# The second layer's latent projection as three passes of high and low parts with 512 weight columns streaming

## The chip, the cores and the metric

The kernel runs on one core of a Trainium2 chip. The metric is device time in microseconds (us) of one execution, the median of several. Five engines work side by side, each through its own instructions in order: PE (TensorE, matrix products into PSUM; PEld are its weight loads), DVE (VectorE), ACT (ScalarE), POOL (GpSimd, which issues the gathers) and SP (SyncE, which issues most loads).

## The reference, cut to what matters

Two transformer-like layers are run for two groups that share all weights: 128 context tokens (block 0) and 256 latent tokens (blocks 1 and 2). D is 1024, everything is float32. In each layer

```
h   = LN(x) * (1 + scale1) + shift1
q_a, k_a, v_a, cq, ckv, krope, u_c, v_c = split(h @ w_in)      # 1024 x 1696, the projection
q_a = rms(q_a) * g;  k_a = rms(k_a) * g;  latent tokens also get a rotary turn (rope)
mix = concat(GQA 8 heads, latent attention (MLA) 4 heads, gated MLP) @ w_o
x   = LN(alpha * x + gate1 * mix)
x   = LN(alpha * x + gate2 * PEER(LN(x) * (1 + scale2) + shift2))
```

PEER scores 16 x 128 keys per token (`h2 @ peer_wq`, queries), takes the best pairs (routing) and mixes 128 of 16384 single-neuron experts. For the latent tokens the kernel runs all experts densely on PE; for the context tokens it gathers the chosen rows of two tables.

## The kernel before, in words

Tokens stand 128 to a partition block. A layer has two stages. The first is attention: the latent chain (`lat`, blocks 1 and 2) and the context chain (`cc`, block 0) run interleaved. Each does: LN and transpose (`transposed_mod`, L193, gives `hT`, the transposed h, 8 chunks of 128 x 128 per block), projection (`project`, L247), attention (L341), output projection (`out_proj`, tiles `psoc`, `psol`), LN. The context chain then runs its queries (L552, tile `psqp`), routing (L573) and 128 + 128 gathers (L679) with a DVE product for each gathered row. The second stage is the dense expert work of the latent tokens (L852 and L926, tiles `psA` and `acc`), with the context's gathers spread between.

`project` before: the 1696 columns of `w_in` come in 13 strips of 128 and one of 32. A strip is one load of 128 x 1024 float32 (all 8 chunks of the contraction, 128 columns each) into one of `RB` = 6 ring buffers that all loads on SP share. For each block, 8 float32 matmuls (L262, the transposed h stationary, the 128 weight columns streaming) sum into one PSUM bank (`psil` for the latent blocks, `psic` for the context), and ACT copies the strip out to `proj` (L263). So after five strips the 640 columns of q and k are there, and `norm_qk` (L295: square on ACT, sum, reciprocal root, three products, rope on DVE) can start on them.

The ring buffer of a strip comes free when the matmuls of both blocks have read it. The context chain of the second layer has a small ring of its own (`cr1`, two buffers).

The order on each engine is not the order of the code: a list scheduler (`schedule_with_timeline_sim`, L1119) places instructions by priority and by its own simulated times, and `hp()` gives the context chain a higher priority. `ORD1` ('paol...') sets the code order: the context's projection, attention and output projection first, then the 14 steps of the latent projection, to which the scheduler gives the gaps. The latent attention's tiles lie in a pool `lb1` that is opened on the right-hand side of SBUF after the projection's code.

The dense expert stage already splits float32 numbers into a high part (a copy to the type float32r, ACT) and a low part (the difference, DVE) and does three matmuls in place of one: high by high, low by high, high by low (L915, L916, L926).

Of the kernel before, what the change touches and what calls it, by code (L numbers as in the profile page):

```python
# [8 lines left out]
F32 = mybir.dt.float32  # L9
F32R = mybir.dt.float32r  # L10
# [3 lines left out]
AF = mybir.ActivationFunctionType  # L14
# [10 lines left out]
IN_W = sum(SIZES)  # L25
# [20 lines left out]
def tile_fn(ctx: ExitStack, tc, A, outs):  # L46
    nc = tc.nc
    V, S, T = nc.vector, nc.scalar, nc.tensor
# [23 lines left out]
    def run(g, n=None):  # L72

        for k, _ in enumerate(g):
            if n is not None and k + 1 == n:
                return
# [170 lines left out]
    def project(l, ch):  # L247

        ch.hT = {b: ch.P.tile([128, 8, 128], F32, name=f"hT{b}", tag=f"hT{i}") for i, b in enumerate(ch.bs)}
        for b in ch.bs:  # L250
            with crit(b):
                transposed_mod(b, l, 1, 0, lambda h: ch.hT[b][:, h * 4:h * 4 + 4, :], "m1", ch.P, ch.tT)
        ch.proj = {b: ch.P.tile([128, IN_W], F32, name=f"proj{b}", tag=f"proj{i}") for i, b in enumerate(ch.bs)}
        for j in range(14):
            w0 = j * 128
            n = min(128, IN_W - w0)
            wv = load(A["w_in"][l, :, w0 * 8:(w0 + n) * 8], f"wi{ch.g}{j}", n * 8, ch.cring)
            wv = wv.rearrange("p (c n) -> p c n", c=8)
            for b in ch.bs:
                ps = pS(ch.tS, "psi" + ch.g)  # L260
                for c in range(8):
                    T.matmul(ps[:, :n], lhsT=ch.hT[b][:, c, :], rhs=wv[:, c, :], start=(c == 0), stop=(c == 7))  # L262
                S.activation(ch.proj[b][:, w0:w0 + n], ps[:, :n], AF.Copy)  # L263
            if j == 9 and ch.ctxg:
                p0 = ch.proj[0]
                nc.scalar.dma_start(o_v[0, l].rearrange("s k d -> s (k d)"), p0[:, O_V:O_V + 128])
                nc.scalar.dma_start(o_kr[0, l], p0[:, O_KR:O_KR + 32])
            yield j

    class Chain:  # L270

# [478 lines left out]
    for l in range(DEPTH):  # L750
        last = l + 1 == DEPTH

        with ExitStack() as es3:
            psum(es3, BK[min(l, 1)])
            with ExitStack() as esc:
                Pc = pool(esc, f"cb{l}")
                if l:
                    with hp():
                        ctx_close(l - 1, pk, Pc)
                Pl = pool(es3, f"lp{l}", side="right")  # L760
                Wl = Shared(l, Pc, Pl)
                if l:
                    Wl.load()
                lat = Chain(l, [1, 2], Pl, Wl)
                cc = Chain(l, [0], Pc, Wl, pool(esc, f"cr{l}") if l else None)
                pl_ = project(l, lat)
                def first():
                    run(project(l, cc))
                    if l == 0:
                        with tc.issue_after(hmark[-1].ins):  # L770
                            Wl.load()
                            for t, n in late:
                                nc.scalar.dma_start(t, A[n])

                st_ = {"p": first, "2": lambda: modulation(0, 2, "m"),
                       "4": lambda: modulation(0, 4, "m"), "3": lambda: modulation(0, 3, "m"),
                       "a": lambda: cc.attention_in(esc), "o": lambda: out_c(cc)}
                for k in (ORD if l == 0 else ORD1):
                    if k == "l":
                        run(pl_, 1)  # L780
                    else:
                        with hp():
                            st_[k]()
                with hp():
                    pk = ctx_picks(l, cc, esc)
                run(pl_)
                if not last:
                    mods = [(l + 1, v) for v in (1, 0, 2, 4, 3, 5)]
                    for _ in range(MB):
                        modulation(*mods.pop(0), "m")  # L790
                lat.attention(pool(es3, f"lb{l}", side="right"))
                lat.out_proj()
                if l == 0:
                    modulation(0, 5, "m")

        with ExitStack() as es_:
# [32 lines left out]
            for b in (1, 2):  # L829
# [3 lines left out]
                for h in range(2):  # L833
                    hs = slice(h * 4, h * 4 + 4)
# [97 lines left out]
            for b in range(2):  # L932
                g, i1, i2 = routing(l, vals[b], idx[b], PK, PK)
                ps = pS("t", "psr")
# [48 lines left out]
            for b in (1, 2):  # L983
# [3 lines left out]
                with crit():  # L987
                    for h in range(2):
                        hs = slice(h * 512, (h + 1) * 512)
# [7 lines left out]
            for k, r in RATES[l].items():  # L997
                ms = marks[k]
                n = int(len(ms) * r + 0.5)
# [47 lines left out]
def _layout(i):  # L1047
    import numpy as np
    i = {k: np.asarray(v) for k, v in i.items()}
    L = i["w_mod"].shape[0]  # L1050
    f = np.float32
    r = {}

    def chunks(w, n):
        k = w.shape[2] // n
        return w.reshape(L, 8, 128, k, n).transpose(0, 3, 2, 1, 4).reshape(L, k, 128, 8 * n)
# [10 lines left out]
    t = np.arange(256)  # L1067
# [20 lines left out]
    r["w_mod"] = i["w_mod"].reshape(L, 8, 128, 6, D).transpose(0, 3, 1, 2, 4)  # L1088
    wi = i["w_in"].reshape(L, 8, 128, IN_W).transpose(0, 2, 1, 3)
    r["w_in"] = np.concatenate([wi[:, :, :, j * 128:(j + 1) * 128].reshape(L, 128, -1) for j in range(14)], -1)  # L1090
    r["w_o"] = chunks(i["w_o"], 128)
    r["peer_wq"] = chunks(i["peer_wq"], 128)
    r["peer_uT"] = i["peer_u"].reshape(L, 128, 128, 8, 128).transpose(0, 1, 4, 3, 2).reshape(L, 128, 128, 1024)
# [29 lines left out]
```

## Time and profile before

| | us |
|---|---|
| three runs | 2402.37, 2407.3, 2410.01 |
| median | 2407.3 |
| the profiled execution, its own time | 2407.9 |
| its span | 2406.1 |
| PE busy | 2260.6 (94%) |
| DVE busy | 1904.6 (79%) |
| ACT busy | 1115.2 (46%) |

The second layer's projection of both chains runs from about 1222 to 1342 us of the span, the rest of the attention stage to about 1500, and the expert stage from there to the end. A row of a timeline gives start, duration, engine, line, operation, tile and its inputs, shape, count, and in brackets the idle time ahead of it; a row by stretch gives the stretch, its length, the busy us (and records) of PE, PEld, DVE, ACT and POOL, PE's granted clock, the DMA share and GB/s. A matmul of float32 shows as two records in the trace. Matmuls are pipelined, so the durations of single records overlap; the chain of waits gives the time that a group of them takes one after the other. Busy PE is time with a matmul in flight, at whatever pace.

### The profile page before, as it was taken

How to read it: one execution, taken by the hardware profiler on the slowest of the kernel's cores; microseconds unless marked ns; L12 is line 12 of the kernel's file. 1: busy time of each engine (PE TensorE's matmuls, PEld its weight loads, DVE VectorE, ACT ScalarE, POOL GpSimd, SP SyncE). 2: the span in 40 equal slices, each digit the busy share in tenths (PEclk: the TensorE clock that was granted, in tenths of full speed). 3: DMA queues.
4: the chain of work that ended last, by engine and by line, in shares of the span. 5: the costliest groups of instructions: out<-in, count | busy, mean ns of one | idle time of the engine just before them, and what ended most of it. 6: DMA issues, size and time to landing. Idle time of an engine off the chain costs nothing.

```text
span 2406.1 us, 41658 instructions
## 1 busy us (share of the span) xinstructions
PE 2260.6 (94%) x15660; PEld 1914.5 (80%) x15660; DVE 1904.6 (79%) x3942; ACT 1115.2 (46%) x2084; POOL 697.7 (29%) x523
## 2 busy tenths in 40 slices
PE   6999889999999999999989996989999999998997
PEld 5686469999998995667778785889999889855886
DVE  3157579996898888898863468899879888899987
ACT  3324532442785445444445553134348744444444
POOL 0000233454004433464200003435530143344630
PEclk8999989999999999999999998999999999998998
DMA  9967889999658999999863355989985599987994
GB/s 331 322 193 265 336 322 348 324 358 350 219 159 295 360 332 347 328 352 374 299 213 113 120 158 196 325 313 349 363 320 159 188 374 346 333 309 270 395 364 147
DMA packets 196314, 696.05 MB, mean 289 GB/s; under 512 B 22992, under 2 KB 27408, under 8 KB 196112
## 3 DMA queue, kind: packets, MB, share of 16 engines
q1 hardware_dynamic: 110016, 398.52, 46.7%
q0 software_dynamic: 74736, 272.14, 31.1%
q10 hardware_dynamic: 11360, 22.73, 2.8%
q8 instruction: 123, 2.02, 0.3%
q14 instruction: 79, 0.65, 0.1%
HBM read 689.14 MB, written 4.16 MB: 288 GB/s over the span
## 4 chain that ended last, share of the span: by engine, by line
PE 32%; DVE 8%; issue 8%; DMA 2%; POOL 1%; ACT 1%; DVEq 0%; ACTq 0%; POOLq 0%
PE acc L926 18%; PE psA L852 6%; DVE gt L692 2%; PE psil L262 2%; DMA gt<-in_peer_u_dram,ids 1%; POOL gt L686 1%; PE psqp L561 1%; PE psic L262 1%; DVE ulo L847 1%; PE psoc L522 1%; PE pssl L421 1%; DMA wic<-in_w_in_dram 1%; PE psW L890 0%; DVE idx L550 0%; DVE rep L548 0%
## 5 line engine op out<-in xcount | busy, mean ns | idle before, releaser
L686 POOL DMA_INDIRECT gt<-in_peer_u_dram,ids x256 | 325.3, 1271 | 1185.6 <-DVE gt L692 478.4
L686 POOL DMA_INDIRECT gt<-in_peer_v_dram,ids x256 | 368.0, 1438 | 464.0 <-DVE acc L703 434.7
L926 PE MATMUL acc<-vhi,pp 128*128 128x512 f32 x1728 | 441.9, 398 | 15.6 <-ACT pp L906 9.4
L852 PE MATMUL psA<-h2hi,uhi 128*128 128x256 f32 x1664 | 416.2, 287 | 5.1 <-ACT uhi L846 5.1
L852 PE MATMUL psA<-h2lo,uhi 128*128 128x256 f32 x1664 | 411.3, 284 | 0.0
L926 PEld LDWEIGHTS acc<-vhi,pp 128*128 128x128 f32 x1728 | 326.1, 191 | 86.3 <-ACT pp L906 10.0
L915 ACT ACTIVATE vhi<-v 128x1024 fp32r<-128x1024 f32 x216 | 228.7, 1060 | 274.0 <-PE acc L926 161.2
L692 DVE SCALAR_TENSOR_TENSOR gt<-gt,h2c 128x1024 f32<-128x1024 f32 x256 | 309.5, 1216 | 28.0 <-DMA gt<-in_peer_u_dram,ids 27.9
L703 DVE SCALAR_TENSOR_TENSOR acc<-gt,wcol,acc 128x1024 f32<-128x1024 f32 x254 | 325.5, 1282 | 6.2 <-DMA gt<-in_peer_v_dram,ids 5.2
L846 ACT ACTIVATE uhi<-u 128x1024 fp32r<-128x1024 f32 x208 | 220.0, 1058 | 230.2 <-PE psA L852 107.5
L852 PEld LDWEIGHTS psA<-h2hi,uhi 128*128 128x128 f32 x1664 | 319.7, 192 | 7.9 <-ACT uhi L846 5.7
L852 PEld LDWEIGHTS psA<-h2lo,uhi 128*128 128x128 f32 x1664 | 320.0, 192 | 2.1
L847 DVE TENSOR_TENSOR ulo<-u,uhi 128x1024 fp32r<-128x1024 f32 x208 | 254.3, 1223 | 79.9 <-ACT uhi L846 74.7
L916 DVE TENSOR_TENSOR vlo<-v,vhi 128x1024 fp32r<-128x1024 f32 x216 | 263.6, 1223 | 52.6 <-ACT vhi L915 47.7
L852 PE MATMUL psA<-h2hi,ulo 128*128 128x256 f32 x1664 | 239.4, 286 | 1.0 <-DVE ulo L847 0.8
L926 PE MATMUL acc<-vlo,pp 128*128 128x512 f32 x864 | 234.3, 392 | 1.5 <-DVE vlo L916 1.4
L852 PEld LDWEIGHTS psA<-h2hi,ulo 128*128 128x128 f32 x1664 | 216.2, 192 | 3.0 <-DVE ulo L847 1.6
L872 ACT ACTIVATE e<-iota,nid 128x128 f16<-128x128 f16 x512 | 158.9, 426 | 112.1 <-PE psW L890 112.1
L926 PEld LDWEIGHTS acc<-vlo,pp 128*128 128x128 f32 x864 | 162.3, 189 | 35.8 <-DVE vlo L916 2.5
L852 PE MATMUL psA<-h2T,u 128*128 128x256 f32 x768 | 171.8, 379 | 0.0
L852 PEld LDWEIGHTS psA<-h2T,u 128*128 128x128 f32 x768 | 143.1, 190 | 18.1
L926 PE MATMUL acc<-v,AR 128*128 128x512 f32 x320 | 143.6, 599 | 0.0
(437 smaller groups left out, 3039.9 us busy)
## 6 DMA issues: line engine op xcount, KB each, us to landing
u<-in_peer_uT_dram SPq DMA_DIRECT2D x256, 512.0 KB, 6.0
v<-in_peer_v_dram SPq DMA_DIRECT2D x256, 512.0 KB, 6.0
wm<-in_w_mod_dram SPq DMA_DIRECT2D x96, 512.0 KB, 7.2
wq<-in_peer_wq_dram SPq DMA_DIRECT2D x64, 512.0 KB, 4.7
wic<-in_w_in_dram SPq DMA_DIRECT2D x26, 512.0 KB, 5.7
wil<-in_w_in_dram SPq DMA_DIRECT2D x26, 512.0 KB, 4.2
woc<-in_w_o_dram SPq DMA_DIRECT2D x16, 512.0 KB
wol<-in_w_o_dram SPq DMA_DIRECT2D x16, 512.0 KB, 3.6
```

Source lines behind the costliest of these rows:

```text
L262: T.matmul(ps[:, :n], lhsT=ch.hT[b][:, c, :], rhs=wv[:, c, :], start=(c == 0), stop=(c == 7))
L421: T.matmul(sb[i][:, m * nk:(m + 1) * nk], lhsT=lhs(i, h), rhs=rhs(h), start=True, stop=True)
L686: nc.gpsimd.indirect_dma_start(out=t, out_offset=None, in_=tab, in_offset=bass.IndirectOffsetOnAxis(ap=pk.ids[:, j:j + 1], axis=0))
L692: V.scalar_tensor_tensor(t, t, 1.0, pk.h2c, op0=OP.mult, op1=OP.mult, accum_out=acol[:, j:j + 1])
L703: V.scalar_tensor_tensor(pk.acc, t, wcol[:, j:j + 1], pk.acc, op0=OP.mult, op1=OP.add)
L846: S.activation(hi, ua, AF.Copy)
L847: marks["A" if ii < NA else "U" if ii < NA + PRE else "B"].append(V.tensor_sub(lo, ua, hi.bitcast(F32)))
L852: T.matmul(ps[:, a * 256:(a + 1) * 256], lhsT=lw[:, c * 128:(c + 1) * 128], rhs=rw[:, c, :], start=(k == 0), stop=(k == len(passes) - 1))
L872: S.activation(e2[:, t // TI, :, t % TI], iota1, AF.Abs, bias=nb_[:, t0 % 128 + t:t0 % 128 + t + 1])
L915: S.activation(hi, v, AF.Copy)
L916: marks["O" if ii >= NA else "Q" if ii >= NA - PRE else "P"].append(V.tensor_sub(lo, v, hi.bitcast(F32)))
L926: T.matmul(accp[tb][h], lhsT=pl[:, tb * 128:(tb + 1) * 128], rhs=vr[:, h * 512:(h + 1) * 512], start=st0, stop=sp)
```

## The change

Only the second layer's latent projection changes; the first layer and the context keep `project`. The new `project_split` takes the weights from a second copy `w_in5` in DRAM, laid out in three groups of 512 columns and one of 160. A load brings two chunks of the contraction by 512 columns (128 x 1024), or four chunks by 160 (128 x 640). For the groups of 512 the load is split into `wjhi` (ACT copy to float32r) and `wjlo` (DVE difference), two buffers each, and the transposed h into `hThi` and `hTlo`. For each chunk and block three matmuls of 512 streaming columns follow (high h by high w, low h by high w, high h by low w), and the sum of all eight chunks is copied out in one piece of 512 columns per block. The last 160 columns stay float32. The new tiles lie in a pool `pj1` on the right-hand side that is closed before `lb1` is opened, so that `lb1` takes its place.

```diff
+    def project_split(l, ch, P2):
+        ch.hT = {b: ch.P.tile([128, 8, 128], F32, ...) for i, b in enumerate(ch.bs)}
+        hl = {}
+        for b in ch.bs:
+            with crit(b):
+                transposed_mod(b, l, 1, 0, lambda h: ch.hT[b][:, h * 4:h * 4 + 4, :], "m1", ch.P, ch.tT)
+                hi = P2.tile([128, 8, 128], F32R, name=f"hThi{b}")
+                lo = P2.tile([128, 8, 128], F32R, name=f"hTlo{b}")
+                for h in range(2):
+                    hs = slice(h * 4, h * 4 + 4)
+                    S.activation(hi[:, hs], ch.hT[b][:, hs], AF.Copy)
+                    V.tensor_sub(lo[:, hs], ch.hT[b][:, hs], hi[:, hs].bitcast(F32))
+                hl[b] = (hi, lo)
...
+        for q in range(4):
+            w0, n, m = q * 512, (512 if q < 3 else IN_W - 1536), (2 if q < 3 else 4)
+            ps = {b: pS(t, "psi" + ch.g) for b, t in zip(ch.bs, (ch.tS, ch.tT))}
+            for k in range(8 // m):
+                o = w0 * 8 + k * m * n
+                wv = load(A["w_in5"][l, :, o:o + m * n], f"wj{q}{k}", m * n)
+                if q < 3:
+                    wh = P2.tile([128, 1024], F32R, name="wjhi", tag="wjhi", bufs=2)
+                    wl = P2.tile([128, 1024], F32R, name="wjlo", tag="wjlo", bufs=2)
+                    S.activation(wh, wv, AF.Copy)
+                    V.tensor_sub(wl, wv, wh.bitcast(F32))
+                for b in ch.bs:
+                    if q < 3:
+                        ops = [(x_, wh, c) for c in range(m) for x_ in hl[b]] + [(hl[b][0], wl, c) for c in range(m)]
+                    else:
+                        ops = [(ch.hT[b], wv, c) for c in range(m)]
+                    for u, (x_, w_, c) in enumerate(ops):
+                        T.matmul(ps[b][:, :n], lhsT=x_[:, k * m + c, :], rhs=w_[:, c * n:(c + 1) * n], ...)
+                yield q
+            for b in ch.bs:
+                S.activation(ch.proj[b][:, w0:w0 + n], ps[b][:, :n], AF.Copy)
...
-                pl_ = project(l, lat)
+                esk = es3.enter_context(ExitStack())
+                pl_ = project_split(l, lat, pool(esk, f"pj{l}", side="right")) if l else project(l, lat)
...
                 run(pl_)
+                esk.close()
```

The scheduler then orders the whole second layer anew. On PE, at the place where the first latent block has its transposed h and the second has not yet (`psT`, `pssc`, `psk` and `pso_` are pieces of the context's attention, `m1pst` the transposes of the second block's h), the row stood so before:

```order
L421 MATMUL pssc<-kTc,qTc 128x128 x4
L201 MATMUL m1pst<-ident,m1xh 128x128 x8
L262 MATMUL psil<-wil_13107,hT_13040 128x128
L262 MATMUL psil<-wil_13129,hT_13039 128x128 x8
L262 MATMUL psil<-wil_13107,hT_13040 128x128 x6
L221 MATMUL psk<-ident,kd 128x128 x2
L436 MATMUL psT<-ident,pt 128x128
```

and now, at the end of the first block's first twelve matmuls:

```order
L302 MATMUL psil<-wjhi,hThi_13076 128x512
L302 MATMUL psil<-wjhi,hTlo_13077 128x512
L302 MATMUL psil<-wjlo,hThi_13076 128x512 x2
L459 MATMUL pssc<-kTc,qTc 128x128 x4
L201 MATMUL m1pst<-ident,m1xh 128x128 x8
L474 MATMUL psT<-ident,pt 128x128 x4
L302 MATMUL psil<-wjhi,hThi_13114 128x512
```

Projection matmuls of the first block stood between `m1pst` and `psT`; now none does, since the next weights need a buffer that the second block still has to read.

On PE at the end of the projection (`pssl` are the latent attention's scores, `psoc` the context's output projection, `psck`, `pskv`, `pskm` the preparation of the cached keys) it ended so before:

```order
L522 MATMUL psoc<-woc_12920,mTc 128x128
L450 MATMUL pso__12900<-pT,vmc 64x128
L262 MATMUL psil<-wil_13393,hT_13039 128x32 x8
L262 MATMUL psil<-wil_13393,hT_13040 128x32 x4
L450 MATMUL pso__12900<-pT,vmc 64x128
L262 MATMUL psil<-wil_13393,hT_13040 128x32 x4
L421 MATMUL pssl<-kTl,qTl 128x384
```

and now, behind the last projection matmul:

```order
L221 MATMUL psck<-ident,cache 128x128
L411 MATMUL pskv<-w_ukv,ckT 128x512
L221 MATMUL pskm<-ident,km 96x128 x4
L221 MATMUL psmx<-ident,oc 128x128 x2
L459 MATMUL pssc<-kmTc,qmTc_12715 128x128 x4
L221 MATMUL psk<-ident,kd 128x128 x2
L474 MATMUL psT<-ident,pt 128x128 x3
L221 MATMUL psk<-ident,kd 128x128 x2
L221 MATMUL psq<-ident,proj_13120 128x128 x4
L474 MATMUL psT<-ident,pt 128x128
L221 MATMUL psq<-ident,proj_13121 128x128 x4
L459 MATMUL pssl<-kTl,qTl 128x384
```

The cached keys, the context's MLA scores and the transposes of the latent keys and q (`psk`, `psq`), which stood among the projection's matmuls, now stand behind them; the context's four `pso_` products of the MLA heads and its first five `psoc` matmuls stand behind the first `pssl`.

On ACT, the squares of the latent q and k (`sq`) with which `norm_qk` begins stood so before, when eight of the first block's thirteen full strips were still to be copied:

```order
L222 COPY kmTl<-pskm 96x4x128
L300 ACTIVATE sq<-proj_13105 128x640
L452 COPY mTc<-pso__12800 64x128
L222 COPY ckT<-psck 128x128
L263 ACTIVATE proj_13106<-psil 128x128
L300 ACTIVATE sq<-proj_13106 128x640
L263 ACTIVATE proj_13105<-psil 128x128
L115 ACT_TABLE_LOAD
```

and now:

```order
L306 ACTIVATE proj_13120<-psil 128x512
L222 COPY cqT<-pscq 128x256
L306 ACTIVATE proj_13121<-psil 128x512
L338 ACTIVATE sq<-proj_13120 128x640
L306 ACTIVATE proj_13120<-psil 128x160
L338 ACTIVATE sq<-proj_13121 128x640
L115 ACT_TABLE_LOAD
```

The two squares moved behind the copy of the third and last group of 512 columns: `sq` lies in the pool `lb1`, whose place `pj1` holds until then.

## Rows read from the trace of the kernel before

**Rows 1.** The page's first part: busy us, share of the span, instructions.

```profile
PE 2260.6 (94%) x15660; PEld 1914.5 (80%) x15660; DVE 1904.6 (79%) x3942; ACT 1115.2 (46%) x2084; POOL 697.7 (29%) x523
```

**Rows 2.** Busy time by stretch of the span; PEclk is the granted clock.

```profile
1266.00:1279.00 13.00, 10.99 (x91) 10.08 (x91) 4.08 (x13) 10.08 (x32) 0.00 (x0) 1.00 0.38 120
1279.00:1323.00 44.00, 44.00 (x353) 40.06 (x352) 18.11 (x47) 21.52 (x72) 0.00 (x0) 1.00 0.37 114
1323.00:1341.00 18.00, 18.00 (x145) 16.85 (x143) 3.73 (x20) 5.36 (x17) 0.00 (x0) 0.95 0.38 121
...
1474.00:1500.00 26.00, 10.91 (x84) 9.94 (x82) 22.06 (x49) 8.04 (x21) 14.93 (x14) 0.79 0.92 339
...
1560.00:1700.00 140.00, 133.10 (x870) 124.56 (x869) 138.84 (x450) 55.28 (x68) 65.70 (x48) 0.98 0.92 334
```

**Rows 3.** Chain that ended last: start, duration, work (two records per float32 matmul).

```profile
1179.81 35.60 PE acc L926 x157
...
1289.19 1.79 PE psil L262 x16
```

**Rows 4.** PE timeline: the projection's head, and its strip of 32 columns.

```profile
1270.72 1.09 PE L201 MATMUL m1pst<-ident,m1xh 128*128 128x128 f32 x8
1271.92 2.50 PE L262 MATMUL psil<-wil,hT 128*128 128x128 f32 x20
1275.44 1.60 PE L262 MATMUL psil<-wil,hT 128*128 128x128 f32 x10 [1.02 <-ACT hT L209]
...
1277.55 0.49 PE L436 MATMUL psT<-ident,pt 128*128 128x128 f32 x3
...
1335.94 2.87 PE L262 MATMUL psil<-wil,hT 128*128 128x32 f32 x24
```

**Rows 5.** ACT timeline: softmax of the context, `norm_qk`.

```profile
1275.60 1.30 ACT L430 ACTIVATE pt<-pt,sums 128x128 f32<-128x128 f32 x4
...
1278.07 0.59 ACT L437 COPY pT<-psT 128x512 f32<-128x512 f32 x1
...
1294.28 0.74 ACT L300 ACTIVATE sq<-proj 128x640 f32<-128x640 f32 x1
...
1298.29 1.28 ACT L115 ACT_TABLE_LOAD   x1
```

**Rows 6.** DVE timeline: `norm_qk` and rope of the latent blocks.

```profile
1297.28 0.82 DVE L301 TENSOR_REDUCE ss<-sq 128x10 f32<-128x640 f32 x1 [1.42 <-ACT sq L300]
...
1300.78 1.56 DVE L307 TENSOR_TENSOR proj<-proj,rn 128x640 f32<-128x640 f32 x2
...
1308.81 0.82 DVE L293 TENSOR_TENSOR proj<-rp,rp 128x640 f32<-128x640 f32 x1
```

**Rows 7.** The page's groups: the existing split of the expert weights.

```profile
L915 ACT ACTIVATE vhi<-v 128x1024 fp32r<-128x1024 f32 x216 | 228.7, 1060 | 274.0 <-PE acc L926 161.2
...
L916 DVE TENSOR_TENSOR vlo<-v,vhi 128x1024 fp32r<-128x1024 f32 x216 | 263.6, 1223 | 52.6 <-ACT vhi L915 47.7
```

**Rows 8.** PE timeline: first latent scores, last context queries, last `psol`, second block's transposes.

```profile
1340.95 1.65 PE L421 MATMUL pssl<-kTl,qTl 64*128 64x384 f32 x2
...
1434.04 1.95 PE L561 MATMUL psqp<-h2Tc,wq 128*128 128x128 f32 x16
...
1482.54 2.05 PE L522 MATMUL psol<-wol,mTl 128*128 128x128 f32 x16 [0.82 <-DVE y L524]
...
1504.75 1.97 PE L201 MATMUL m2pst<-ident,m2xh 128*128 128x128 f32 x8 [7.13 <-ACT m2xh L149]
```

**Rows 9.** POOL timeline: the first gather of the second layer's context.

```profile
1473.86 0.94 POOL L686 DMA_INDIRECT gt<-in_peer_u_dram,ids  x1 [296.10 <-DVE y L524]
```

**Rows 10.** Chain that ended last, the latent attention's pieces and the end.

```profile
1355.29 1.98 PE psoc L522 x16
...
1358.44 1.44 PE pso__14088 L450 x6
...
2213.78 176.49 PE acc L926 x765
```

More of the change, by code (lines that the diff above doesn't have):

```diff
@@ L268, in project @@
             yield j
+    def project_split(l, ch, P2):
+        ch.hT = {b: ch.P.tile([128, 8, 128], F32, name=f"hT{b}", tag=f"hT{i}") for i, b in enumerate(ch.bs)}
+        hl = {}
[9 more added lines that the diff above has]
+                hl[b] = (hi, lo)
+        ch.proj = {b: ch.P.tile([128, IN_W], F32, name=f"proj{b}", tag=f"proj{i}") for i, b in enumerate(ch.bs)}
+        for q in range(4):
[15 more added lines that the diff above has]
+                    for u, (x_, w_, c) in enumerate(ops):
+                        T.matmul(ps[b][:, :n], lhsT=x_[:, k * m + c, :], rhs=w_[:, c * n:(c + 1) * n],
+                                 start=(k == 0 and u == 0), stop=(k == 8 // m - 1 and u == len(ops) - 1))
+                yield q
+            for b in ch.bs:
+                S.activation(ch.proj[b][:, w0:w0 + n], ps[b][:, :n], AF.Copy)
     class Chain:
@@ L1090, in _layout @@
     r["w_in"] = np.concatenate([wi[:, :, :, j * 128:(j + 1) * 128].reshape(L, 128, -1) for j in range(14)], -1)
+    r["w_in5"] = np.concatenate([wi[:, :, :, q * 512:(q + 1) * 512].reshape(L, 128, -1) for q in range(4)], -1)
     r["w_o"] = chunks(i["w_o"], 128)
```

## The prediction

> **What bounds the kernel now.** I read the page's first part first: PE is busy for 94% of the span, DVE for 79%, ACT for 46% [rows 1]. So PE time that is taken away could come off the end, and ACT and DVE have room on average. The rows by stretch tell more than the averages [rows 2]. From 1279 to 1323 us, in the middle of the second layer's projection, PE is full (44.0 of 44), with DVE at 18.1 and ACT at 21.5. From 1323 to 1341 it is full too. From 1474 to 1500, behind the attention, PE is busy for only 10.9 of 26 us, and there it waits for the latent LN: the last `psol` ends at about 1484.6, the transposes of the second block end at 1506.7 [rows 8]. From 1560 to 1700 DVE is the full one (138.8 of 140). The chain that ended last runs through the projection (`psil` x16, 1.79 us) and closes with 176.5 us of PE's `acc` [rows 3, 10]. Two chains leave the attention stage: the latent one, whose end starts the dense expert stage, and the context's, whose last queries are on PE at 1434 and whose first gather is issued at 1473.9 [rows 8, 9]. Gathers and their DVE products feed the stretch in which DVE is full. A gain in the projection reaches the end only if both chains get it.
>
> **PE, removed and added.** Thirteen full strips, two blocks, eight chunks make 208 float32 matmuls of 128 columns. Eight of them (x16 records) take 1.79 us [rows 3], 0.2238 us each: 46.5 us. The strip of 32 columns has 16, of which 12 (x24) take 2.87 us [rows 4], 0.24 each: 3.8 us. Removed: 50.3 us. Added are 3 groups x 8 chunks x 2 blocks x 3 passes = 144 matmuls of 512 columns in float32r. The `acc` matmuls of the expert stage have that type and width (one record each): 157 in 35.60 us [rows 3], 0.2268 each, so 32.7 us. Then 16 float32 matmuls of 160 columns, not in the trace; by columns from the 128 wide ones 0.2238 x 160/128 = 0.28 each, 4.5 us (between 3.6, if they cost as 128 columns, and 7.2 at twice that). Net: 50.3 - 32.7 - 4.5 = 13.1 us less, between 10.4 and 14.0.
>
> On the 512-column matmul the Trainium skill ("TensorE: Matmul & The Clock Gate", Part 2, "Step-by-step: what each phase is for") has 215.7 ns from start to start at full clock. The row shows 226.8 ns, 5% more, in a stretch that carries the same weight loads. By the page's figure the added work would be 144 x 0.2157 = 31.1 us, 1.6 us less; the row decides.
>
> **ACT and DVE.** Twelve loads of 1024 are split: 12 x 1.06 = 12.7 us on ACT and 12 x 1.22 = 14.7 us on DVE [rows 7]. The split of the transposed h is four halves of 512 columns; at half the row, about 0.6 each, that is 2.4 us on each engine. ACT copies eight wide pieces in place of 28 narrow ones; the narrow ones aren't shown, a 512-wide copy takes 0.59 [rows 5], so I leave this at no change. Against the 62 us from 1279 to 1341, of which ACT is free for 35 and DVE for 40 [rows 2], this fits. One load's split (ACT, then DVE, 2.3 us in a row) feeds 12 matmuls, 2.7 us on PE, with two buffers of each. It is hidden if ACT and DVE take it in turn with their other pieces, a piece of up to 1.6 us [rows 6]. If that cover fails, each of the twelve loads may stand PE still for about 0.5 us, up to 6 us in all; I count 1.
>
> **The head.** Between the `m1pst` transposes and `psT` stood 15 projection matmuls of the first block (x20 and x10, 2.50 + 1.60 us less overlap, about 3.4 us by 0.2238) [rows 4]. None is left there, since the third load's high part waits for a buffer that the second block still has to read, and its transposed h comes only behind `m1pst`. `psT` itself can't come earlier than 1277.5: it waits for the context's softmax, on ACT until 1276.9 [rows 5]. So PE stands there for 3.4 us of work that is then still to be done. I take 4, between 2 and 6.
>
> **The tail.** `norm_qk` and rope ran beside the projection: the first square at 1294.28, the last rope product over at 1309.63 [rows 5, 6], 15.4 us, of which 1.4 waited for a square. Now both squares lie behind the last group of 512 columns, since their pool takes the place of `pj1`. What the projection then still has for PE is little. Other pieces, nearly all the context's, held 62 - (50.3 - 5.4) = 17 us of PE between 1279 and 1341, where 5.4 is the projection's work ahead of 1279 (the 3.4 above and about 2 ahead of `m1pst`). From 1279 the rest of the 144 (132, 30.0 us), the 4.5 of the last columns and about half of those 17 us give 1279 + 30.0 + 4.5 + 8.5 = 1322, say 1323 for the projection's end against about 1341 before. The last `sq` can't start until about 1320; with two copies (0.6 each), the chain of 15.4 less its wait, and about 2 us for the keys' and q's transposes and copies, the first `pssl` comes at 1320 + 1.2 + 14 + 2 = 1337, against 1340.95 [rows 8]. In between PE has the other half, about 8.5 us, less what was moved behind `pssl`: 4 `pso_` (x6 records, 1.44 us for 3 [rows 10], so 1.9) and 5 `psoc` (8 take 1.98, so 1.2), 3.1 us. So 5.4 us of work in 14: PE is idle for some 8 us just ahead of the first `pssl`, though DVE and ACT aren't.
>
> **The sum.** Of 13.1 us, 4 go in the head, 1 in the splits, 8 less the overlap with the 18 us by which the projection ends earlier in the tail; what arrives is read at `pssl`: 4 us earlier, with 3.1 us more work behind it. That is about 1 us at the latent end. Against that stands the finer mixing behind `pssl`, where ACT and DVE come out of the projection with nothing overdue, worth perhaps 1 to 2 us: latent end 2.5 us earlier. For the context its `psoc` and queries stand behind the same latent pieces as before, which come earlier, and its own five `psoc` later: last queries at 1434 + 1 to 2. The dense stage starts about 2.5 us earlier, the gathers about 1.5 later, and the stretch with DVE full takes the mean of both: -1 us. Profiled execution 2407.9 - 1 = 2407; the median lies 0.6 under the profiled one: 2406.
>
> **Rivals.** The forecast is no change: 2406, its own range 2400 to 2414 (gaps in head and tail smaller or larger by 6 us). A measurement of this kernel tells about 0.3% (7.2 us) from no change.
>
> Faster: PE finds work in both gaps. For it: the context's output projection stands behind the first `pssl` and could be drawn on, DVE and ACT are free for half of the projection, and the idle 8 us were worked out from its own order rather than from a row. If half of the gaps is filled, 13.1 - 1 - 2 - 1.5 = 9 arrive: 2398; with all, 13.1: 2394. Against it: order on an engine is fixed, and the rows of the order show none of it there.
>
> Slower: the context's chain decides. The price has its place at the idle PE ahead of the first `pssl`. After the idle stretch 1474 to 1500 the rows show a granted clock of 0.79, which is a mean of the two levels, 1.2 and 2.4 GHz [rows 2]. The 8 us of sparse PE at about 1329 to 1337 can do the same: at 1.2 GHz the pieces behind it take twice as long, some 3 to 4 us. With 3.1 us moved behind `pssl`, and the context's queries queued behind them, the first gather comes some 8 us later than 1473.9, and from 1560 on DVE, full, has no room to make it good: 2416. It decides once the last context queries are later than about 1442. Against it: ids come 38 us after the queries, which leaves other work in which a delay can be taken back.
>
> The Trainium skill ("TensorE: Matmul & The Clock Gate", Part 1, "HAM oscillation — how this bites in real kernels") says that gaps between groups of matmuls put the array back to half its clock and that the work behind each gap starts cold. The 0.79 in the row of 1474 to 1500 agrees with it; that it would do so at this smaller gap no row shows.
>
> The change does not do what it says: if a float32r matmul of 512 columns went at the float32 rate here (0.2238 x 4 = 0.9 us), 144 would cost 129 us, and the time would be about 2500. The expert stage's rows speak against it.
>
> **How the numbers follow.** No change 0.48, faster by the gaps being filled 0.28, slower by the context's chain 0.22, not as it says 0.02. The range takes in most of the first three: 2395 to 2418. Faster by over 0.3% is below 2400.1: 0.29, with a tail of the forecast's own; slower is above 2414.5: 0.24; within, 0.47.
>
> **What would show it.** Right: `psil` of 512 columns at 0.225 to 0.23 us each; the last projection matmul near 1323; PE idle for 6 to 10 us between it and the first `pssl`, which stands at 1335 to 1339; last context queries at 1434 to 1438, first gather within 3 us of 1473.9. A gap that is filled (first `pssl` before 1332) means the faster case. The granted clock under 0.9 behind the gap, and last queries after 1442, mean the slower one. Splits that PE waits for in the middle of the projection, by more than 0.5 us a load, would make the price of ACT and DVE wrong. Wrong altogether: a projection that takes as long as before.

## The result and the profile after

| | before | after |
|---|---|---|
| median of five runs, us | 2407.3 | 2423.7 |
| lowest and highest | 2402.4, 2412.2 | 2422.0, 2430.2 |
| ratio, 95% interval | | 1.0072 [1.005, 1.0093] |
| span of the profiled execution | 2406.1 | 2421.9 |

The change makes the kernel slower by 16 us; the forecast was no change, 2406, and its range ended at 2418. The first thing to read is where the two traces part. The PE timelines have the end of the first layer's expert stage, a place up to which the order is the same on every engine, as the last `acc` row ahead of the second layer's stage. Before:

```profile
1237.40 0.61 PE L926 MATMUL acc<-vlo,pp 128*128 128x512 f32 x2
```

After:

```profile
1247.28 0.61 PE L966 MATMUL acc<-vlo,pp 128*128 128x512 f32 x2
```

So 9.9 us of the difference arose where nothing was changed; experiment e1 shows that the first layer can scatter by about as much without the change. From here on all times are taken **from the end of that last `acc`** (1238.0 and 1247.9 us). From there to the end of the program it is 1168.1 before and 1174.0 after: the second layer's own loss in these two profiles is 5.9 us.

The stretch from there to the last `psol`, by busy time (columns as in [rows 2]), and the latent attention's part of it. Before:

```profile
1238.00:1484.60 246.60, 230.43 (x1665) 195.25 (x1663) 141.35 (x511) 118.53 (x330) 5.86 (x7) 0.98 0.43 136
...
1341.00:1436.00 95.00, 91.87 (x582) 70.61 (x582) 55.02 (x202) 51.17 (x135) 0.00 (x0) 0.96 0.47 149
```

After, then its parts that answer to [rows 2]: the head, the projection, the tail, the attention, the wait for the LN; the last two rows are stretches with half clock, in the head and in the attention:

```profile
1247.90:1497.40 249.50, 222.87 (x1392) 176.41 (x1391) 152.61 (x519) 127.09 (x328) 0.50 (x1) 0.95 0.40 127
...
1276.00:1289.00 13.00, 9.07 (x40) 6.52 (x39) 5.35 (x15) 11.62 (x37) 0.00 (x0) 0.84 0.41 149
1289.00:1333.00 44.00, 44.00 (x195) 33.48 (x195) 18.32 (x28) 20.33 (x43) 0.00 (x0) 0.93 0.40 124
1333.00:1351.00 18.00, 11.40 (x60) 8.24 (x59) 14.13 (x53) 14.63 (x41) 0.00 (x0) 0.91 0.17 57
1351.00:1446.00 95.00, 88.54 (x547) 64.91 (x546) 50.95 (x179) 48.62 (x132) 0.00 (x0) 0.95 0.40 127
1484.00:1510.00 26.00, 15.30 (x128) 14.74 (x126) 20.37 (x53) 8.73 (x18) 5.89 (x7) 0.81 0.63 216
...
1288.30:1295.10 6.80, 6.43 (x18) 4.83 (x19) 2.49 (x5) 3.83 (x13) 0.00 (x0) 0.50 0.24 75
1390.70:1404.30 13.60, 10.30 (x30) 5.19 (x28) 8.09 (x20) 4.42 (x12) 0.00 (x0) 0.63 0.19 64
```

The two long rows (the first of each fence) are the account of this stretch. PE was idle for 246.6 - 230.4 = 16.2 us before and 249.5 - 222.9 = 26.6 after: **10.4 us more idle**. PE's busy time fell by 7.6 us only, though 13.0 us of work at full clock went (the prediction's 13.1; the 160 wide strip measured 0.286 us each instead of 0.28): **5.4 us were lost to the clock**, whose mean in this stretch went from 0.98 to 0.95. -13.0 + 10.4 + 5.4 = +2.8, and the stretch is 2.9 us longer. The 5.4 is what is left over, so it needs a second reading: the clock's record has 10.2 us of this stretch at half clock before and 23.9 after, 13.7 more, and at the price that the pair of e5 below shows (6.5 us for 17) that is an estimated 5.2. The profile of e2, the changed kernel once more, repeats the account: 10.1 us more idle, 6.4 lost to the clock. Behind the last `psol` 3.0 us more are lost up to the end of the program.

The PE timeline after, with the places (head, half clock, full clock, the last projection matmuls, tail, queries, outputs) in order:

```profile
1283.20 1.09 PE L201 MATMUL m1pst<-ident,m1xh 128*128 128x128 f32 x8
1286.93 1.20 PE L474 MATMUL psT<-ident,pt 128*128 128x128 f32 x4 [2.63 <-ACT pt L468]
1288.66 0.79 PE L302 MATMUL psil<-wjhi,hThi 128*128 128x512 f32 x1 [0.54 <-ACT hThi L281]
...
1292.60 0.63 PE L302 MATMUL psil<-wjhi,hThi 128*128 128x512 f32 x1
1293.03 0.63 PE L302 MATMUL psil<-wjhi,hTlo 128*128 128x512 f32 x1
...
1309.41 0.39 PE L302 MATMUL psil<-wjhi,hTlo 128*128 128x512 f32 x1
1309.64 0.39 PE L302 MATMUL psil<-wjhi,hThi 128*128 128x512 f32 x1
...
1330.61 3.15 PE L302 MATMUL psil<-wj,hT 128*128 128x160 f32 x22
...
1344.80 0.44 PE L221 MATMUL psk<-ident,kd 128*128 128x128 f32 x2 [2.67 <-ACT kd L401]
...
1350.67 0.91 PE L459 MATMUL pssl<-kTl,qTl 64*128 64x384 f32 x2 [1.26 <-ACT qTl L222]
...
1453.54 1.95 PE L599 MATMUL psqp<-h2Tc,wq 128*128 128x128 f32 x16
...
1482.81 14.56 PE L560 MATMUL psol<-wol,mTl 128*128 128x128 f32 x128 [0.67 <-DVE y L562]
...
1519.07 1.97 PE L201 MATMUL m2pst<-ident,m2xh 128*128 128x128 f32 x8 [9.99 <-ACT m2xh L149]
```

Here one sees what a half clock is: at 1292.6 the 512-column matmuls start 0.43 us apart, at 1309.4 they start 0.23 apart. It follows on the wait of 2.63 us for the context's softmax. Another 3.4 us at half clock lie ahead of that wait (1278.0 to 1281.4); e2 has none there, but 6.8 us of it still earlier. The tail on ACT, where the squares wait for the third group, and on DVE:

```profile
1331.36 0.75 ACT L338 ACTIVATE sq<-proj 128x640 f32<-128x640 f32 x1
...
1333.18 0.73 ACT L338 ACTIVATE sq<-proj 128x640 f32<-128x640 f32 x1
1333.92 1.28 ACT L115 ACT_TABLE_LOAD   x1
```

```profile
1345.31 0.82 DVE L331 TENSOR_TENSOR proj<-rp,rp 128x640 f32<-128x640 f32 x1
```

From the first square to the last rope product it is 14.8 us, as before (15.4 [rows 5, 6]), but now with little else for PE. And the context's first gather on POOL, which stood at 1473.86 [rows 9]:

```profile
1496.90 0.94 POOL L724 DMA_INDIRECT gt<-in_peer_u_dram,ids  x1 [309.25 <-DVE la_rs L118]
```

### The profile page after: what moved, and what is told of

It is laid out like the page before. It is cut to its first block, busy times and chain, and to the rows that moved or that the text cites. A ratio compares the mean times of both kernels' runs of the same rounds, so it can differ in the third digit from the quotient of the medians.

```text
span 2421.9 us, 41129 instructions
## 1 busy us (share of the span) xinstructions
PE 2258.9 (93%) x15388; PEld 1899.3 (78%) x15388; DVE 1918.3 (79%) x3954; ACT 1124.9 (46%) x2082; POOL 688.3 (28%) x523
## 4 chain that ended last, share of the span: by engine, by line
PE 28%; issue 10%; DVE 7%; DMA 3%; POOL 2%; ACT 1%; ACTq 0%; DVEq 0%; POOLq 0%
PE acc L966 14%; PE psA L892 6%; POOL gt L724 2%; DMA gt<-in_peer_u_dram,ids 2%; PE psil L302 2%; DVE gt L730 2%; PE psqp L599 1%; DMA gt<-in_peer_v_dram,ids 1%; PE psic L262 1%; PE pssl L459 1%; PE psoc L560 1%; DVE ulo L887 1%; DVE acc L741 0%; PE psT L480 0%; DVE y L215 0%
## 5 line engine op out<-in xcount | busy, mean ns | idle before, releaser
L724 POOL DMA_INDIRECT gt<-in_peer_v_dram,ids x256 | 359.5, 1404 | 473.0 <-DVE acc L741 429.7
L966 PE MATMUL acc<-vhi,pp 128*128 128x512 f32 x1728 | 441.8, 398 | 15.4 <-ACT pp L946 9.9
L966 PEld LDWEIGHTS acc<-vhi,pp 128*128 128x128 f32 x1728 | 325.8, 191 | 85.9 <-ACT pp L946 10.4
```

What stands on the lines that cost most here:

```text
L724: nc.gpsimd.indirect_dma_start(out=t, out_offset=None, in_=tab, in_offset=bass.IndirectOffsetOnAxis(ap=pk.ids[:, j:j + 1], axis=0))
L966: T.matmul(accp[tb][h], lhsT=pl[:, tb * 128:(tb + 1) * 128], rhs=vr[:, h * 512:(h + 1) * 512], start=st0, stop=sp)
```

## The experiments

The table gives for every profile, from the end of the last first-layer `acc`, the start of the last `m2pst` matmul (the latent chain's end), the first gather and the end of the program; PE's idle time and mean clock from there to the last `psol`, read as above; and the ratio of all timed runs (10 to 12, of e6 and e7 six, against 23 to 35 of the kernel before on the same chip; for "after" five against five). A profile is one execution: that of e1 and that of e3 were the slowest of their twelve, that of e4 the fastest.

| | acc ends | m2pst | gather | end | idle | clock | ratio |
|---|---|---|---|---|---|---|---|
| before | 1238.0 | 268.3 | 235.9 | 1168.1 | 16.2 | 0.98 | |
| after | 1247.9 | 272.7 | 249.0 | 1174.0 | 26.6 | 0.95 | 1.0072 |
| e1 before, second copy | 1246.6 | 267.2 | 234.6 | 1168.6 | 16.2 | 0.99 | 0.9997 [0.9985, 1.0009] |
| e2 copy last | 1245.6 | 273.2 | 249.6 | 1176.7 | 26.3 | 0.95 | 1.0042 [1.0025, 1.0059] |
| e3 own place | 1253.3 | 275.6 | 246.8 | 1175.4 | 20.6 | 0.92 | 1.0026 [1.0012, 1.004] |
| e4 other bank | 1240.5 | 265.7 | 235.4 | 1167.9 | 24.2 | 0.96 | 1.0008 [0.9996, 1.002] |
| e5 place and bank | 1244.1 | 258.9 | 242.5 | 1161.5 | 20.6 | 0.97 | 1.0004 [0.999, 1.0019] |
| e5 again | 1241.2 | 265.5 | 248.8 | 1170.8 | 20.4 | 0.94 | 1.0001 [0.9988, 1.0013] |
| e6 one pass, other bank | 1240.0 | 250.0 | 226.4 | 1153.5 | 26.5 | 0.94 | 0.9945 [0.9924, 0.9966] |
| e7 four buffers, other bank | 1240.1 | 277.8 | 261.3 | 1180.5 | 27.4 | 0.91 | 1.0066 [1.0044, 1.0089] |
| e8 before, bank held | 1241.1 | 267.0 | 234.6 | 1166.5 | 16.4 | 0.99 | 1.0015 [0.9998, 1.0031] |
| e9 after, head filled | 1245.9 | 273.9 | 249.7 | 1172.3 | 23.4 | 0.94 | 1.0035 [1.0019, 1.0051] |
| e10 groups of 256 | 1240.4 | 265.8 | 249.6 | 1169.6 | 23.2 | 0.96 | 1.0011 [0.9999, 1.0022] |
| e11 plain 512 | 1241.0 | 266.5 | 256.8 | 1170.1 | 19.6 | 0.98 | 1.0023 [1.0009, 1.0037] |
| e12 e5, latent first | 1244.7 | 267.4 | 257.5 | 1171.7 | 20.8 | 0.94 | 1.0014 [0.9999, 1.0028] |
| e13 before, latent first | 1244.7 | 272.1 | 255.6 | 1172.6 | 17.9 | 0.97 | 1.0029 [1.0014, 1.0045] |
| e14 e5, head filled | 1240.5 | 261.8 | 245.1 | 1162.8 | 20.6 | 0.97 | 0.9995 [0.998, 1.001] |

**Is the first layer's 9.9 us the second copy's doing?** e1 adds the copy of the weights to the kernel before (`+ r["w_in5"] = ...`), e2 moves that line to the end of the layout.

> The kernel before, unchanged in its instructions, with the second copy of the weights lying in DRAM behind w_in as in the changed kernel, unread. In the profiles the changed kernel is 9.9 us late already at the end of the first layer (context's second projection pair at 1241.4 against 1231.5 us), where both kernels have the same order on every engine. Theory P (the extra 13.9 MB move the tensors behind w_in to other places in DRAM and loads land later): 2415 to 2419 us, the pair at about 1241. Theory S (the 9.9 us are scatter of loads in one execution, or come from something else in the changed kernel): 2404 to 2411 us, the pair within 3 us of 1231.

> The changed kernel with the second copy as the last tensor, so that the others lie as before. Theory P: the first layer gets its 9.9 us back, about 2414 us (what is left is the second layer's own loss of 6 us). Theory S: 2420 to 2428 us as the changed kernel, whatever its first layer shows in one profile.

Both decide for theory S, in time: e1 is the kernel before by its ratio. Its 2412.9 us lie in neither range, since the kernel before itself took 2412.4 on that chip, and its profile has the sign of theory P: `acc` ended at 1246.6, 8.6 us later than in the first one. But e8, with the same first layer again, ended at 1241.1, and e2, with the copy last, at 1245.6. So the first layer scatters by some 9 us from one execution to the next. e2 is 10 us slower than before (6 to 14), of which its profile shows 8.6 in the second layer. Its median, 2423.7 us, is that of the changed kernel above; it is the kernel before that took 2407.3 there and 2411 to 2412 later, of 23 to 35 runs. So 10 us is the better figure for the change, and 5.9 and 8.6 of it stand in the second layer's profiles. The rest is open: the four profiles with the changed kernel's bank (after, e2, e3, e9) have first layers that end at 1245.6 to 1253.3, later than all the others but e1's, and whether that is chance is not settled.

**The tail and the bank.** e3 gives the small tiles of the latent attention a place of their own, e4 changes a PSUM bank, e5 does both.

```diff
+                lbr = pool(es3, f"lr{l}", side="right") if l else None    # e3, e5
-                lat.attention(pool(es3, f"lb{l}", side="right"))
+                lat.attention(pool(es3, f"lb{l}", side="right"), lbr)
-            ps = {... zip(ch.bs, (ch.tS, ch.tT))}
+            ps = {... zip(ch.bs, (ch.tS, ch.tO))}                         # e4, e5
```

> The changed kernel, but the small tiles of the latent attention (squares, rope, keys, values) have a place of their own, so that the squares and the key's preparation need not wait for the end of the projection; only softmax tiles and the MLA queries stay in the place of pj1. Theory T (the tail, norm_qk behind the projection, is what costs in the second layer): first pssl 6 to 10 us earlier, last context queries 6 to 10 us earlier, time 2414 to 2418 us. Theory B (the transposes of the latent chain share the PSUM bank that the sums of 512 columns hold for a whole group, and this spoils the mixing): little gain, 2420 to 2425 us.

> The changed kernel with the second block's sums of 512 columns in the bank that the latent attention uses later (tag o), in place of one of the two banks of the transposes (tag t). Theory B: the context's and the keys' transposes stand among the projection again, last context queries 5 to 10 us earlier, 2414 to 2419 us. Theory T: the squares stay behind the projection, 2420 to 2426 us.

> Own place (e3) and other bank (e4) together. Measured from the end of the first layer's acc, the first gather came 235.9 us on in the kernel before, 249.0 in the changed one, 246.8 with the own place, 235.4 with the other bank; the end 1168.1, 1174.0, 1175.4 and 1167.9. Theory B (the bank alone spoils the context, the tail is a second loss of its own): gather at 233 to 237, first pssl at 95 to 98 instead of 104, latent end 3 to 6 us earlier, end 1162 to 1166, ratio 0.996 to 1.000. Theory C (whatever latent work is let out early stands in the context's way): gather at 240 to 250 as in e3, ratio 1.001 to 1.005.

> e5 once more. If its profile was typical: m2pst within 2 us of 258.9, end within 2 us of 1161.5 from the first layer's end, and the time 0.996 to 0.999 of before. If it was a lucky one: m2pst at 262 to 268, end 1164 to 1169, time 0.999 to 1.002.

e4 came as theory B said: last context queries (198.0 against 207.3, and 197.7 before), gather and end as in the kernel before, but no better. In time it is 10 us faster than e2 on the same chip (2413.8 against 2423.7), so the loss went with the bank. Its stretch to the last `psol`:

```profile
1240.50:1483.90 243.40, 219.25 (x1393) 175.09 (x1391) 151.82 (x518) 129.95 (x329) 4.68 (x5) 0.96 0.41 134
```

Against the kernel before that is 8.0 us more idle and, of the 13.0 us of work, 11.2 less busy: 1.8 lost to the clock instead of 5.4. e3 did what it should to the tail (first `pssl` at 95.8 instead of 102.8, idle 6 us less), but the last context queries came no earlier (208.9), and its profile was not faster: its clock was 0.92. Its median, 2418.9 us, lies between the two theories' ranges, and its interval overlaps that of e2. e5 has the earlier tail, with a gather as theory C had it, and in its first profile seemed to win 6.6 us. The same program once more shows why that is no gain. The stretch to the last `psol` of e5:

```profile
1244.10:1481.80 237.70, 217.12 (x1393) 175.83 (x1392) 146.93 (x509) 123.14 (x325) 0.00 (x0) 0.97 0.40 129
```

and of e5 again:

```profile
1241.20:1485.20 244.00, 223.61 (x1393) 180.23 (x1392) 146.91 (x509) 123.83 (x325) 0.00 (x0) 0.94 0.39 125
```

The same 1393 matmul records, the same idle time (20.6 and 20.4), but 6.5 us more busy, and 6.3 us longer. The clock's record has 13.7 us at half clock in the one and 30.7 in the other: 17 us of half clock cost 6.5 us. In its times e5 is not distinguishable from the kernel before.

**Does PE's work count at all?** e6 is e4 with the high by high pass alone.

```diff
-  ops = [(x_, wh, c) for c in range(m) for x_ in hl[b]] + [(hl[b][0], wl, c) for c in range(m)]
+  ops = [(hl[b][0], wh, c) for c in range(m)]
```

> e4 with the high by high pass alone (leaves out the two passes with low parts, so the result has only the high parts' accuracy): 96 matmuls of 512 columns less, 21.8 us of PE. Theory W (PE's work bounds the stage): first pssl, last context queries and the end all come 12 to 22 us earlier, ratio 0.991 to 0.995. Theory L (latencies bound it: norm_qk behind the projection, the context's own chain): the projection ends some 18 us earlier, of which half at most reaches the first pssl and less than 5 us the first gather; ratio 0.997 to 1.000.

It does: of 21.8 us of work less than e4, 14.4 arrive at the end (1167.9 to 1153.5), theory W, and the ratios of the two are 0.6% (15 us) apart. So the 13 us that the change saves would be worth some 8.6 at this rate, an estimate; idle time and clock took them.

**Head and buffers.** e7 is e4 with `bufs=4` for `wjhi` and `wjlo`. e9 and e14 add 12 idle matmuls (`fill`, 128 columns, reading a piece of the second block's transposed h) in the head, to the changed kernel and to e5; they are meant for PE's wait there. In e9 they stand in it; in e14 the scheduler placed them behind it.

> e4 with four buffers each for the high and low parts of the weights in place of two, so that the splits can run ahead of the second block's transposed h and the first block's matmuls fill PE in the head. Theory H (the head's gap costs, as the prediction said, about 4 us): projection ends 3 to 5 us earlier, end 1 to 4 us earlier than e4, ratio 0.998 to 1.000. If the gap is hidden by what comes later: within 2 us of e4, ratio 0.999 to 1.002.

> The changed kernel with 12 idle float32 matmuls of 128 columns (2.7 us, into a spare bank, read by nobody) where PE stands still in the head, between the second block's m1pst and the context's psT. In the two profiles of the three-pass kernel that wait was followed by 6.8 us at a granted clock of 0.5, in which 512-column matmuls started 0.43 us apart instead of 0.227. Theory K (idle costs twice, by itself and by the half clock behind it): the 6.8 us at half clock go, the projection ends 2 to 4 us earlier from the end of the first layer's acc than 87.4, the latent transposes (m2pst) 2 to 4 us earlier than 272.7, end 1170 to 1172; ratio 1.002 to 1.005. Rival (the clock falls there anyway): projection's end within 1 us of 87.4, end 1173 to 1177.

> e5 with 12 idle matmuls (2.7 us) in the head as in e9. Theory K: the half clock behind the second block's m1pst (6.8 us in e5) goes, projection ends 3 to 6 us earlier than 88.1, and with the tail gone too this reaches the latent end: m2pst 253 to 257, ratio 0.995 to 0.999. Rival (the clock falls later instead, as in e9, where it was at half for 22.8 us behind the first pssl): m2pst 258 to 264, ratio 0.999 to 1.002.

e7 is the clearest miss: 12.6 us worse than e4, with 44.4 us at half clock, the most of all. Its ACT timeline has the four splits in a row ahead of the transposed h, and the second block's LN 6 us later than in e4 (1277.5 against 1271.5, with the `acc` ends 0.4 us apart); that the one makes the other is read from the timeline, not tested:

```profile
1261.71 3.89 ACT L294 ACTIVATE wjhi<-wj 128x1024 fp32r<-128x1024 f32 x4
...
1277.48 1.25 ACT L149 ACTIVATE m1xh<-xl,m_q,m_rs 128x1024 f32<-128x1024 f32 x1
```

In e9 the idle matmuls fill the wait, and the projection runs at full clock at once:

```profile
1281.30 2.94 PE L307 MATMUL fill<-hT,ident 128*128 128x128 f32 x24 [1.69 <-ACT hT L209]
...
1286.36 0.39 PE L302 MATMUL psil<-wjhi,hThi 128*128 128x512 f32 x1
1286.59 0.39 PE L302 MATMUL psil<-wjhi,hTlo 128*128 128x512 f32 x1
```

The projection ended at 81.4 instead of 87.4, more than theory K said, and took 53.4 us from its first to its last matmul instead of 58.2 (57.1 in e2). But the gain did not last. The next 48 us of e9 and the 44 behind them, by stretch, and then the 44 of the changed kernel that answer to these:

```profile
1280.00:1328.00 48.00, 46.52 (x233) 36.36 (x234) 21.62 (x41) 26.90 (x63) 0.00 (x0) 1.00 0.40 135
1328.00:1372.00 44.00, 37.18 (x153) 23.36 (x152) 23.59 (x76) 27.60 (x75) 0.00 (x0) 0.73 0.15 51
...
1330.00:1374.00 44.00, 37.36 (x217) 26.61 (x216) 27.94 (x92) 30.68 (x82) 0.00 (x0) 0.96 0.27 88
```

Full clock in the head, then 0.73 across the tail and the first latent scores, where the changed kernel had 0.96; the clock was at half for 23.9 us, from 8 us ahead of the first `pssl` on. m2pst was no earlier (273.9), against theory K, and the end, 1172.3, lies between the two theories. In e14 PE still waits, and the idle matmuls come behind it:

```profile
1277.59 0.47 PE L478 MATMUL psT<-ident,pt 128*128 128x128 f32 x1 [2.92 <-ACT pt L472]
1277.86 3.56 PE L307 MATMUL fill<-hT,ident 128*128 128x128 f32 x18
```

So e14 is no trial of a filled wait; its m2pst of 261.8 falls to the rival. With tail and bank mended as well, it has the best time of the three-pass kernels, 0.9995, which is the kernel before.

**Which part of the change makes the idle time?** e8 holds one of the two `t` banks through the old projection (one transpose in, one copy out); e10 is e5 with groups of 256 columns; e11 is e5 with plain float32 matmuls of 512 columns, without any split.

> The kernel before, in which one of the two banks of the latent transposes is held from the start of the second layer's latent projection to its end (one transpose into it, one small copy out of it, under 1 us of work). Theory B: with the old projection too the order gets worse, context queries and first gather 5 to 13 us later from the end of the first layer, ratio 1.002 to 1.006. Rival (the bank only hurts together with groups of 512 columns, whose 24 matmuls in a row the context waits behind): gather within 3 us of 235.9, ratio 0.999 to 1.002.

> e5 (own place and other bank) with six groups of 256 columns and one of 160 in place of three of 512: as much split work, twice as many matmuls of half the width. q and k are complete after 768 of 1696 columns instead of 1024. Theory T (the tail): first pssl 2 to 5 us earlier than 90.3, latent end (m2pst) 2 to 5 us earlier than 258.9, ratio 0.996 to 0.999. Rival (latent pieces that come earlier are then paid with the context's behind them on PE, as from e4 to e3): m2pst 258 to 263, ratio 0.999 to 1.002.

> e5 with the weights in groups of 512 columns as they are: plain float32 matmuls of 512 columns, no split and no second and third pass. PE's work is that of the kernel before, 13.1 us more than in e5. Theory G (the grouping by itself makes the order worse): PE idle over 20 us and half clock over 13 us from the first layer's end to the last psol, as in e5, m2pst at 270 to 275, ratio 1.002 to 1.006. Theory X (the splits on ACT and DVE are what makes PE wait): idle and half clock as before (16 and 7 to 10 us), m2pst at 266 to 269, ratio 0.999 to 1.001.

The bank alone costs nothing with the old strips (e8; its ratio of 1.0015 has 1 in the interval, and its profile is the kernel before). Narrower groups don't help (e10: the rival's ratio, but first `pssl` at 98.4 and m2pst later than both ranges). e11 is mixed: its 10.2 us at half clock and its m2pst are theory X's, its idle time is just short of theory G's and its ratio is G's. With the groups and no split it is idle for 19.6 us, against 16.2 before and 20.6 with all the splits:

```profile
1241.00:1484.50 243.50, 223.87 (x1345) 164.67 (x1343) 131.29 (x489) 113.75 (x310) 0.00 (x0) 0.98 0.39 130
```

So 3.4 of the 4.4 us by which e5 is more idle than the kernel before come with the grouping and the order that follows from it, without the work on ACT and DVE. The half clock in the head does not: e11 has none there. PE's busy time in e11 is not that of the kernel before, which was expected, but 6.5 us less, with the same 10.2 us at half clock, and still the kernel is not faster. Its projection's matmuls, from its groups:

```profile
L292 PE MATMUL psil<-wj,hT 128*128 128x512 f32 x96 | 43.1, 596 | 0.0
L292 PE MATMUL psil<-wj,hT 128*128 128x160 f32 x32 | 5.2, 306 | 0.0
```

48 matmuls in 43.1 us, 0.90 each: four times the 128-column one, as the prediction's last rival took it for float32; three float32r passes cost 0.68.

**Which chain decides?** e12 and e13 raise the latent attention's priority above the context's, in e5 and in the kernel before (`+ with crit(l):` around `lat.attention`).

> e5 with the latent attention's pieces ahead of the context's in priority (the projection and the latent output projection keep theirs). Theory E (the end follows the latent chain): latent transposes (m2pst) 2 to 10 us earlier than 258.9 from the first layer's end, first gather 10 to 30 us later than 242.5, end 2 to 10 us earlier, ratio 0.994 to 0.999. Theory C (the context decides from some point): end later, ratio 1.002 to 1.010.

> The kernel before with the same priority for the latent attention, without the change. Theory E: m2pst 2 to 10 us earlier than 268.3, gather 10 to 30 us later than 235.9, end as much earlier as m2pst, ratio 0.996 to 0.999. Theory C: end later, ratio 1.002 to 1.010.

The latent end came later, not earlier (m2pst 267.4 in e12, later than in both profiles of e5, and 272.1 in e13), so the priority is no remedy and theory E was not put to the test. Theory C's number came in e13 (1.0029), but with the latent end itself late it says nothing about the context. For the question the table is better: end less m2pst is 898.4 to 905.3 in all 17 profiles, while the gather moves from 226 to 261. e4 and e10 have the same m2pst (265.7, 265.8); e10's gather is 14 us later and its end 1.7 us. So by these profiles the end goes with the latent chain's end, and in this pair the context's delay costs about a tenth of itself.

## Why the prediction was wrong

- **The step that failed: the sum has no term for the clock.** Its work and its idle time came as forecast: 13.0 us less work (13.1), and 10.4 us more idle, where the sum let 13.1 - 2.5 = 10.6 go to head, splits and tail, less what the finer mixing was to give back. By these two alone the last latent `psol` would have come 2.6 us earlier, and 2.5 was forecast. The clock, which the sum put at nothing and only the rival on the context priced (3 to 4 us), took 5.4 us of the stretch, so that it ended 2.9 us later; 3.0 more were lost behind it.
- **Where the clock fell:** not where the rival had it. Around its first `pssl` the kernel before was at half clock already, for 6.8 us from 1339.1 on (the prediction called 1323 to 1341 full and passed over its clock of 0.95 [rows 2]), the changed kernel for 3.4. The additional half clock stands in the head (10.2 us against none) and in the attention (10.2 us, in the row from 1390.7, against 3.4). In the head, between 28 and 52 us, every profile with the split has some, 3.4 to 17 us, but for e9; the four with the old projection and e11 have none. The pair of e5 shows the price of half clock with nothing else changed; e9 ties that of the head to the wait there, in one profile.
- **What the prediction did not look at: the bank.** With the second block's sums in another bank (e4) the clock takes 1.8 us instead of 5.4, the additional idle time is 8.0 instead of 10.4, and the time is that of the kernel before. That moving the bank takes the 10 us back is thus shown (e4, and with the own place e5 and e14); by which step of the scheduler's order it came to idle time and half clock was not traced.
- **First `pssl` 4 us earlier:** wrong. It came at 102.8, as before (102.9); 1337 was forecast and 1341 reached when the first layer's lateness is taken off. The squares stood at 1331.4 instead of 1320 (1321.5 against 1320 on the same footing), the projection's end at 87.4 (1325 against 1323), and from the first square to the first `pssl` it took 19 us instead of 17, with PE waiting 2.67 us for `kd` and 1.26 for `qTl`.
- **Finer mixing worth 1 to 2 us:** wrong. PE's idle time in the attention's row rose from 3.1 to 6.5 us; the last `psol` ended 2.9 us later, m2pst 4.4 later.
- **Last context queries 1 to 2 us later:** wrong, 9.6 later, and the first gather 13.1 later. The place of the block's sums did that (e4: both back), but a held bank does not do it with the old strips (e8).
- **The rival "the context's chain decides":** two of its signs came (queries past the mark, gather 13 us late), the third, a clock under 0.9 behind the gap, did not (0.95 from 1351 to 1446). Nor did its consequence: the end follows m2pst. The result has its direction, but not by its way.
- **The end as the mean of both chains:** wrong, as e4 and e10 show: 14 us in the gather moved the end by 1.7.
- **Right:** the work, 13.0 us (forecast 13.1); 512 columns 0.229 us apart on average at full clock (forecast 0.2268); the projection 18 us shorter (58.2 against 76.6 from its first to its last matmul); the order in head and tail; 6.6 us of idle PE between the projection's end and the first `pssl` (6 to 10); the splits hidden (PE busy for 44.0 of 44 us in the projection's row).

The Trainium skill ("TensorE: Matmul & The Clock Gate", Part 1, "What's actually happening") says that the gate knows two levels and that the number of slow matmuls changes from run to run of one kernel, since its sampling runs free of the program. The rows agree: 0.50 in the narrow stretch, and 13.7 against 30.7 us in two executions of one program.

## What to carry to other kernels

Work taken from a full PE is worth only what remains after the new idle gaps, and each gap on PE may be paid twice: by itself and by matmuls at half clock behind it. Ask of a faster stage whether the smaller pieces that filled it still have something to hide behind, and of a longer sum who else needs the PSUM bank that it holds. Before a gain of 0.3% is believed from a profile, profile the same program twice, and measure from a mark behind the part that wasn't touched.

## What the hardware showed beside that

- Two executions of one program, same order and same idle time, differed by 6.5 us of PE time in 240 by the clock alone.
- A PE that is busy by the records can still fall to half clock: in the kernel before it did so from 1339.1 on, with PE busy without a gap from 1284 to there, at the end with the strip of 32 columns [rows 2, 4]. It did so in e1, e8 and e13 too, the other profiles of the old projection: from 101.1, 99.0 and 101.9 on, in that strip, behind 55 us without a gap. Why is not shown. The row of that stretch in the kernel before:

```profile
1339.10:1345.90 6.80, 6.80 (x27) 5.66 (x27) 3.04 (x13) 3.92 (x7) 0.00 (x0) 0.50 0.61 190
```

- The first layer, with the same order of instructions, ended between 1238.0 and 1253.3 us in 17 profiles.
